# Rotary tables and a norm factor made during the experts, the token update on VectorE alone, and GpSimd given a share of the normalised rows ahead of its low halves

## Chip, cores and metric

One Trainium2 chip; the kernel is one program on one of its cores. The time is device microseconds (us) of one execution, as the median of several. Five engines run at the same time, each through its own instructions in order, and wait for each other by semaphores: TensorE (PE), VectorE (DVE), ScalarE (ACT), GpSimd (POOL) and SyncE (SP), whose queue starts the transfers of the weights.

## The reference, cut

Two transformer-like blocks follow each other on 256 tokens of width 1024, all in float32. The first ends with a mixture of 32 experts; the second begins with a norm, a projection, and rotary tables made from the tokens' positions.

```
def first_block(x, ...):
    ...
        h2 = rmsnorm(x, g_pre_ffn[l]) * (1.0 + sc2) + sh2
        y2 = moe(h2, w_router[l], b_router[l], w_up[l], b_up[l], w_down[l], b_down[l])
        x = x + gt2 * rmsnorm(y2, g_post_ffn[l])
    return x

def rope_tables(positions, rot_dim):
    inv = jnp.power(ROPE_THETA, -(jnp.arange(0, rot_dim, 2, dtype=jnp.float32) / rot_dim))
    ang = positions.astype(jnp.float32)[..., None] * inv
    return jnp.cos(ang)[:, :, None, :], jnp.sin(ang)[:, :, None, :]

def second_block(x, c, positions, ...):
    cos_a, sin_a = rope_tables(positions, ATT_ROT_DIM)
    cos_i, sin_i = rope_tables(positions, IDX_ROT_DIM)
    ...
        mod = jax.nn.silu(c) @ ada_w[l] + ada_b[l]
        shift, scale, gate = jnp.split(mod, 3, axis=-1)
        h = rms_norm(x, norm_g[l]) * (1.0 + scale[:, None, :]) + shift[:, None, :]
        proj = h @ w_in[l]
        (q, k, v, z_att, q_idx, k_idx, w_idx, z_ssm, xbc, dt_raw, gate_logits) = jnp.split(proj, pts, axis=-1)
        ...
        x = x + gate[:, None, :] * (merged @ w_out[l])
```

## The kernel before, in words

**Tokens and weights.** The 256 tokens are two blocks of 128 rows (index i = 0, 1); `xt` holds them, 128 x 2 x 1024. All big weights come in pieces of up to 1 MB through SP's queue, in the order in which they are used, into a ring of buffers; a buffer is filled again when its last reader is done.

**The experts.** A loop over 32 experts e multiplies the tokens that chose e by its two weight matrices. For up to 32 tokens it runs the plain path: eight pieces of `w_up` (`pU`), then the SwiGLU (DVE makes `act`, ACT its tanh `th`, DVE multiplies), then, for expert e - 1, four pieces of `w_down` (`pY`), whose rows DVE and ACT copy to `yz` and PE adds up in `yacc`. If an expert has more than 32 tokens, a branch runs a second chunk of up to 32 right after the SwiGLU (tiles `ov`, `tho`, `pUo`), and if it has more than 64, a third, whose tokens are gathered first (`So` on DVE, `pgo` on PE). Expert 11 takes all three chunks with these inputs.

**The seam.** After the last expert, ACT squares `yacc` and DVE multiplies it by the gate (`yg`). `rstd` computes one over the root of the mean square by DVE alone, with an integer first guess and three Newton steps: a chain of fourteen tiny instructions. Then the tokens are updated, x + rstd * yg: by DVE for three quarters of the columns, and for the last 512 of token block 1 by ACT (scaling) and GpSimd (adding). ACT squares the new tokens for the next norm.

**Block 2** (`block2`) begins with that norm: factor `a3` from the modulation; the first three weight blocks prepared by `early`; a second `rstd`; `norm_rows`, which makes the normalised rows `xn` (in the tile `qkn`), token block 0 by DVE and block 1 by ACT; then, for eight slices k of 128 columns, two PE transposes (`x_T`, tile `pT`) and the two parts of h by `h_halves`: ACT the rounded `h`, DVE `hf` and the remainder `hf` - `h`.

**Splitting.** For float32 accuracy each weight block is split in a rounded high half `wH` (ACT) and a low half `wL` = w - `wH`, and PE makes three products for each. `Flow.halves` decides by a running estimate of loads whether DVE or GpSimd makes a low half. The estimates of both engines start at zero in `block2`, and every instruction that has a price there raises them.

**Order.** `ORDER2` lists the column groups of the projection: first `idx` (the indexer's columns and the step sizes of the state-space part, 324 + 32 columns), then `kv`, `q0` and so on. PE runs them one behind the other. What follows a group runs in "lanes": Python generators that are advanced one step for each weight block, so that their instructions stand between those of the groups. Lane "a" holds first `tables` (the rotary tables `cosin`: eleven table instructions on DVE after a conversion of the positions, and Sin on ACT), then `idx_lane`, which normalises the index key on GpSimd (`kim`, `kiv`, an rsqrt in tile `rsq_t`), applies the rotary tables there, and makes the step sizes (`dtu`, `dtz`). The group `kv` also has a norm, whose rsqrt (`rq`) GpSimd makes behind all of that.

Of the kernel before, what the change touches and what calls it, by code (L numbers as in the profile page):

```python
# [7 lines left out]
F32 = mybir.dt.float32  # L8
F32R = mybir.dt.float32r
BF = mybir.dt.bfloat16  # L10
I32 = mybir.dt.int32
U32 = mybir.dt.uint32
AF = mybir.ActivationFunctionType
OP = mybir.AluOpType
# [6 lines left out]
S, D = 256, 1024  # L21
# [170 lines left out]
class Flow:  # L192
# [11 lines left out]
    def lane(self, q, gen):  # L204
        self.queues[q].append(gen)
# [88 lines left out]
            self.stages()  # L294
        self.pend.clear()

    def early(self, blocks, n, bias=0.0):

        def made():
            for f, w in zip(ws, got):  # L300
                yield None, w
            yield from blocks
        blocks = iter(blocks)
        ws = [next(blocks) for _ in range(n)]
        got = [self.halves(*b) for b in ws]
        for w in got:
            w[0]()
        self.bias, b = bias, self.bias
        for w in got:
            w[1]()  # L310
        self.bias = b
        nop = lambda: None
        got = [(nop, nop, w[2]) for w in got]
        return made()
# [31 lines left out]
def build(tc, A, out):  # L346
    nc = tc.nc
    ACT, SP = nc.scalar, nc.sync
    PE = Load(nc.tensor, PE_PRICES)
    V, G = (Load(e, p, lambda: PE.t) for e, p in ((nc.vector, DVE_PRICES), (nc.gpsimd, POOL_PRICES)))  # L350
    top = ExitStack()
    top.enter_context(tc.manual_schedule())
    con = top.enter_context(tc.tile_pool(name="con", bufs=1))
# [99 lines left out]
    def par(n):  # L453
        return cut(n, (PK, PK0, pk) if n in PK else (PK1, 0, [None, part.get("pk1")]))

    def cs(n):
        return cut(n, (CST, CST0, cst) if n in CST else (CST1, 0, [None, part.get("cst1")]))
# [114 lines left out]
            yield  # L572
        return g

    def norm_rows(xn, x, ss, pool):

        r = pool.tile([128, 2], F32, name="rstd", tag="rstd", bufs=2)
        rstd(r, ss)
        V.tensor_scalar(xn[:, 0], x[:, 0], r[:, 0:1], None, op0=OP.mult)
        ACT.activation(xn[:, 1], x[:, 1], AF.Copy, scale=r[:, 1:2])  # L580

    def x_T(xn, tiles):

# [37 lines left out]
    def blocks(name, ka, extra=None):  # L621

        for j, i in enumerate(at[name]):
            raw = ws.get(i)
            for a in range(ka):
                yield ([raw[:, a]] + ([extra[:, ka * j + a]] if extra is not None else []),
                       (lambda i=i: ws.done(i)) if a == ka - 1 else None)
# [43 lines left out]
        return (lambda: (a[0](), b[0]())), (lambda: (a[1](), b[1]())), lambda: (a[2](), b[2]())  # L671


    def block2(ss=None):
        bk = ExitStack()
        sb = bk.enter_context(tc.tile_pool(name="b2", bufs=1))
# [8 lines left out]
        lane, done, until = fl.lane, fl.done, fl.until  # L685


        a3 = T("a3", [128, 8])
        V.scalar_tensor_tensor(a3, mod2c[:, 8:16], 1.0, par("norm_g2"), op0=OP.add, op1=OP.mult)
        qkn = T("qkn", [128, 16, 256], tag="mg").rearrange("p a b -> p (a b)")[:, :2560].rearrange(  # L690
            "p (i h d) -> p i h d", i=2, h=10)
        xn = qkn.rearrange("p i h d -> p i (h d)")[:, :, :D]
        if ss is None:
            ss = T("ss4", [128, 2])
            for i in range(2):
                ACT.activation(xn[:, i], xt[:, i], AF.Square, accum_out=ss[:, i:i + 1])
        first = fl.early(blocks("idx", 4, par("w_dt").rearrange("p (k c) -> p k c", k=8)), 3, 9.0)
        norm_rows(xn, xt, ss, sb)
        hs = [T(f"h2{i}", [128, 8, 256], F32R) for i in range(2)]

        hk = h_halves(hs, x_T(xn, PG), a3, mod2c[:, 0:8], lambda: T("hf", [128, 512], bufs=2, tag="hjk")[:, :256])


        ri = T("posi", [128, 2], I32)
        ACT.dma_start(ri, A["positions"])
        rp = T("posf", [128, 2])
        cosin = T("cosin", [128, 2, 2, 24])

        def tables():
            V.tensor_copy(rp, ri)  # L710
            ang = T("ang", [128, 2, 24])
            nr = T("nr", [128, 2, 24])
            V.tensor_tensor(ang, cs("invf")[:, None, :].to_broadcast([128, 2, 24]),
                            rp[:, :, None].to_broadcast([128, 2, 24]), op=OP.mult)
            MAGIC = 12582912.0
            V.tensor_scalar(nr, ang, 1.0 / (2.0 * np.pi), MAGIC, op0=OP.mult, op1=OP.add)
            V.tensor_scalar(nr, nr, -MAGIC, None, op0=OP.add)
            c1 = 6.28125
            c2_ = float(np.float32(np.float64(2 * np.pi) - c1))
            c2_ = float(np.float32(np.round(c2_ * 2.0 ** 22) / 2.0 ** 22))  # L720
            c3 = float(2 * np.pi - c1 - c2_)
            for c in (c1, c2_, c3):
                V.scalar_tensor_tensor(ang, nr, -c, ang, op0=OP.mult, op1=OP.add)
            yield
            PI = 3.1415925
            V.tensor_scalar(cosin[:, :, 0], ang, PI, -PI, op0=OP.min, op1=OP.max)
            V.tensor_scalar(ang, ang, float(np.pi / 2), None, op0=OP.add)
            V.tensor_scalar(nr, ang, float(np.pi), float(-2 * np.pi), op0=OP.is_gt, op1=OP.mult)
            V.tensor_tensor(ang, ang, nr, op=OP.add)
            V.tensor_scalar(cosin[:, :, 1], ang, PI, -PI, op0=OP.min, op1=OP.max)  # L730
            yield
            ACT.activation(cosin, cosin, AF.Sin)

        lane("a", tables())

        def rope(x, nh, o, hf):

# [1184 lines left out]
    xn = xq  # L1922
# [94 lines left out]
    def swiglu(U, act, lc, th):  # L2017

        V.tensor_scalar(act, U[:, 0:256], 7.0, None, op0=OP.min)
        V.tensor_scalar(lc, U[:, 256:512], -7.0, 7.0, op0=OP.max, op1=OP.min)  # L2020
        ACT.activation(th, act, AF.Tanh, scale=0.5 * 1.702)  # L2021
        V.scalar_tensor_tensor(act, th, 1.0, act, op0=OP.add, op1=OP.mult)
        V.scalar_tensor_tensor(act, lc, 1.0, act, op0=OP.add, op1=OP.mult)
# [87 lines left out]
    def over_up(e, wu, xT):  # L2111
        with tc.If(rv[e] > 32):  # L2112
            chunk_up(e, lambda k: xT[:, e % 4, k, 32:64], wu, ov[:, 2 * (e % 2)])
            with tc.If(rv[e] > 64):
                x = gather_chunk(e, 2)
                chunk_up(e, lambda k: x[:, k], wu, ov[:, 2 * (e % 2) + 1])
# [29 lines left out]
                far(e, r, b + 1)  # L2146

    aT = {}
    gl = gates_lane()
    for e in range(NE + 1):  # L2150
        if e < NE:
            i0 = at[f"up{e}"][0]
            steps = iter(())
            if e % 4 == 0:
                xT = AR(0, "xT", [128, 4, 8, 64])
                steps = gather(xT, e, min(4, NE - e))
                next(steps)
            U = PU("pU")
            up_bias(e, U)
            act, lc, th = (sb.tile([128, 256], F32, name=n, tag=n, bufs=b) for n, b in (("act", 2), ("lc", 1), ("th", 1)))  # L2160
            if e:
                gs = slots(e - 1, 0, "G", 2)
                next(gs)
            wu = lambda k: ws.get(i0 + k)
            for k in range(8):
                if k % 2 == 0:
                    next(steps, None)
                up_k(U, xT[:, e % 4, k, 0:32], k, wu(k))
                if e == 0 and k < 3:
                    next(gl)  # L2170
                if e and k == 2:
                    g = next(gs)
                if k == 3:
                    rv[e] = nc.values_load(counts[0:1, e:e + 1], engines=(ET.PE, ET.Activation, ET.DVE), min_val=0, max_val=256)
            swiglu(U, act, lc, th)
            over_up(e, wu, xT)
            for j in range(8):
                ws.done(i0 + j)
        if e:
            d0 = at[f"down{e - 1}"][0]  # L2180
            wd = [ws.get(d0 + k) for k in range(4)]
            if e == NE:
                gs = slots(e - 1, 0, "G", 2)
                next(gs)
                g = next(gs)
                gg2, ggc = AR(0, "gg2", [128, D]), sb.tile([128, 8], F32, name="ggc2")
                V.tensor_tensor(ggc, modc[:, 40:48], par("g_post_ffn"), op=OP.mult)
                for _ in row_of(gg2, ggc, at_once(PM)):
                    pass
                over_down(e - 1, wd)  # L2190
            y_out(down(aT[e - 1], wd), yz[e % 2])
        if e < NE:
            aT[e] = sb.tile([128, 2, 128], F32, name="aT", tag="aT", bufs=2)
            act_T(act, aT[e])
        if e:
            scatter(g, yz[e % 2])
            if e < NE:
                over_down(e - 1, wd)
            for k in range(4):
                ws.done(d0 + k)  # L2200
# [13 lines left out]
            V.tensor_tensor(yg[:, i, sl], yacc[i][n], gg2[:, sl], op=OP.mult)  # L2214
    V.tensor_reduce(ss, sq.rearrange("p (i m) -> p i m", m=2), axis=AX.X, op=OP.add)
    rstd(rs, ss)

    q = yg[:, 1, 512:1024]
    ACT.activation(q, q, AF.Copy, scale=rs[:, 1:2])  # L2219
    G.tensor_tensor(xt[:, 1, 512:1024], q, xt[:, 1, 512:1024], op=OP.add)  # L2220
    for i, w in ((0, D), (1, 512)):
        V.scalar_tensor_tensor(xt[:, i, :w], yg[:, i, :w], rs[:, i:i + 1], xt[:, i, :w], op0=OP.mult, op1=OP.add)
        ACT.activation(jk, xt[:, i], AF.Square, accum_out=s3[:, i:i + 1])
    mo.close()
    bx.close()
# [23 lines left out]
```

## Time and profile before

| | us |
|---|---|
| median of 3 runs | 1713.04 |
| lowest and highest run | 1710.18, 1717.36 |
| the profiled execution | 1716.04 |
| its span | 1714.2 |
| PE busy in the span | 1424.8 |
| DVE, ACT, POOL busy | 661.5, 435.9, 271.9 |

The span is what the profiler saw between the first and the last instruction. The experts lie between about 272 and 1270 us of it, where the weights of 32 experts are read; block 2 is what comes behind. The busy shares are means over stages with different limits, so the sections below go by stretches of the span.

### The profile page before, as it was taken

The page shows a single profiled execution, that of the slowest core. Times are in us where ns is not written, and L with a number is a line of the kernel's source. Part 1 is how long each engine was busy: PE and PEld are TensorE (multiplying, and loading weights), DVE is VectorE, ACT ScalarE, POOL GpSimd, SP SyncE. Part 2 cuts the span into 40 slices and gives each one's busy share as a digit, 9 for nine tenths or more (in the row PEclk, how much of TensorE's full clock was granted, in tenths as well). Part 3 has the DMA queues.
Part 4 walks back from the last instruction along what each step waited for, and adds up shares of the span by engine and source line. Part 5 has one row for each costly group of instructions (what it writes and reads, how often), then busy time and mean ns, then how long its engine had stood idle before and what let it go on. Part 6 is the DMA issues. An engine that isn't in the chain of part 4 may idle for free. (4 is left out here: it accounts for less than half of the span.)

```text
span 1714.2 us, 28511 instructions
## 1 busy us (share of the span) xinstructions
PE 1424.8 (83%) x11403; PEld 845.3 (49%) x11403; DVE 661.5 (39%) x1508; ACT 435.9 (25%) x980; POOL 271.9 (16%) x387
## 2 busy tenths in 40 slices
PE   5999988887798898777766778887858888999998
PEld 2775652332233243232132233333227788999996
DVE  3556462121121122121111111221136798766767
ACT  3545331010010011010010010010025555654553
POOL 1127100000000000000000000000005652552533
PEclk8999999999899999889788988999988999999999
DMA  9746896999999988999999998999924344333452
GB/s 377 285 157 219 314 369 267 423 420 422 421 418 420 414 322 353 420 423 421 422 421 421 413 414 336 387 367 420 420 81 148 99 146 144 130 99 113 162 177 91
DMA packets 116487, 526.03 MB, mean 307 GB/s; under 512 B 8744, under 2 KB 11216, under 8 KB 80304
## 3 DMA queue, kind: packets, MB, share of 16 engines
q1 hardware_dynamic: 113392, 518.67, 76.0%
q10 hardware_dynamic: 2496, 3.92, 0.7%
q8 instruction: 157, 2.57, 0.6%
q0 software_dynamic: 384, 0.39, 0.1%
q14 instruction: 58, 0.48, 0.1%
HBM read 521.50 MB, written 1.06 MB: 305 GB/s over the span
## 5 line engine op out<-in xcount | busy, mean ns | idle before, releaser
L145 PE MATMUL pU<-w,xT 128*32 128x512 f32 x2048 | 266.2, 643 | 29.7 <-DMA w<-in_w_up 22.3
L145 PE MATMUL pg<-h,wH 128*128 128x256 f32 x1296 | 249.4, 292 | 9.8 <-ACT wH L254 3.1
L145 DVE TENSOR_TENSOR wL<-w,wH 128x512 fp32r<-128x512 f32 (+2 forms) x244 | 174.2, 728 | 111.1 <-PE pg L145 59.4
L145 PEld LDWEIGHTS pg<-h,wH 128*128 128x128 f32 x1296 | 205.5, 195 | 23.3 <-issue 7.0
L145 PE MATMUL pY<-w,aT 128*32 128x256 f32 x2048 | 151.2, 445 | 73.1 <-PEq L2112 41.3
L254 ACT CAST wH<-w 128x512 fp32r<-128x512 f32 (+4 forms) x312 | 176.1, 587 | 116.0 <-PE pg L145 101.7
L145 PE MATMUL pg<-h,wL 128*128 128x256 f32 (+1 forms) x648 | 186.2, 287 | 6.3 <-DVE wL L145 3.7
L145 POOL TENSOR_TENSOR xt<-yg,xt 128x512 f32<-128x512 f32 x1 | 1.5, 1485 | 1025.9 <-ACT yg L2219 1025.9
L145 PEld LDWEIGHTS pY<-w,aT 128*32 128x32 f32 x2048 | 79.3, 125 | 157.2 <-issue 74.8
L145 PEld LDWEIGHTS pU<-w,xT 128*32 128x32 f32 x2048 | 62.7, 115 | 171.9 <-issue 114.8
L145 DVE COPY yz<-pY 32x256 f32<-32x256 f32 x94 | 39.2, 417 | 248.6 <-PE pY L145 227.6
L145 PEld LDWEIGHTS pg<-h,wL 128*128 128x128 f32 (+1 forms) x648 | 125.7, 194 | 8.0 <-DVE wL L145 4.8
L145 POOL TENSOR_TENSOR wL<-w,wH 128x512 fp32r<-128x512 f32 (+2 forms) x68 | 87.8, 1297 | 222.6 <-PE pg L145 135.7
L2064 ACT COPY yz<-pY 32x256 f32<-32x256 f32 x94 | 34.1, 363 | 304.4 <-DVE yz L145 304.4
L145 PE MATMUL yacc<-yz,G 64*128 64x512 f32 x256 | 91.9, 627 | 17.8 <-ACT yz L2064 17.8
L2021 ACT ACTIVATE th<-act 128x256 f32<-128x256 f32 x32 | 13.3, 416 | 357.8 <-DVE act L145 357.8
L145 PE MATMUL pUo<-w,xT 128*32 128x512 f32 x832 | 92.1, 595 | 0.0
L145 DVE COPY G<-pG 128x256 f32<-128x256 f32 x32 | 13.6, 424 | 183.9 <-PE pG L145 183.9
L145 DVE TENSOR_SCALAR act<-pU 128x256 f32<-128x256 f32 x32 | 13.6, 424 | 155.5 <-PE pU L145 155.5
L145 PE MATMUL pg<-wH,h 128*128 128x512 f32 (+2 forms) x224 | 69.4, 393 | 3.6 <-ACT wH L254 1.9
L145 PE MATMUL pg<-yk,wH 128*128 128x256 f32 x384 | 68.6, 281 | 0.1
L145 PE MATMUL pY<-w,aTo 128*32 128x256 f32 x960 | 54.9, 380 | 9.1 <-DVE Go L145 8.5
(451 smaller groups left out, 1950.1 us busy)
## 6 DMA issues: line engine op xcount, KB each, us to landing
w<-in_w_up SPq DMA_DIRECT2D x256, 1024.0 KB, 17.3
w<-in_w_down SPq DMA_DIRECT2D x128, 1024.0 KB, 19.7
w<-in_w_in SPq DMA_DIRECT2D x48, 1024.0 KB, 4.9
w<-in_w_ada SPq DMA_DIRECT2D x24, 1024.0 KB, 8.5
w<-in_ada_w SPq DMA_DIRECT2D x12, 1024.0 KB, 6.7
w<-in_w_out SPq DMA_DIRECT2D x8, 1024.0 KB, 4.9
w<-in_w_branch_ssm SPq DMA_DIRECT2D x8, 1024.0 KB, 4.9
w<-in_w_branch_att SPq DMA_DIRECT2D x4, 1024.0 KB, 4.9
```

The lines of the kernel that those rows point to most:

```text
L145: return f(*a, **k)
L254: self.nc.scalar.copy(H[:, a:b], p)
L2021: ACT.activation(th, act, AF.Tanh, scale=0.5 * 1.702)
L2064: (ACT.copy if q % 2 else V.tensor_copy)(y[o:o + 32, c:c + 256], t[o:o + 32, 0:256])
```

## The change

Four edits. (1) The factor `a3` and the rotary tables move out of `block2` into a generator `tables`, which the expert loop advances after the SwiGLU of experts 9, 10 and 11: in 9 the factor and the load of the positions, in 10 the first half of the table arithmetic, in 11 the second half and Sin. (2) The token update is made by DVE alone, two instructions of 1024 columns. (3) `norm_rows` is called inside `early`, between the high halves and the low halves of the first three blocks. (4) The last 256 columns of token block 1 are normalised by GpSimd; ACT does 768.

```diff
-    def early(self, blocks, n, bias=0.0):
+    def early(self, blocks, n, bias=0.0, between=None):
...
         for w in got:
             w[0]()
+        if between:
+            between()
         self.bias, b = bias, self.bias
         for w in got:
             w[1]()
...
-    def norm_rows(xn, x, ss, pool):
+    def norm_rows(xn, x, ss, pool, third=0):
...
         V.tensor_scalar(xn[:, 0], x[:, 0], r[:, 0:1], None, op0=OP.mult)
-        ACT.activation(xn[:, 1], x[:, 1], AF.Copy, scale=r[:, 1:2])
+        ACT.activation(xn[:, 1, :D - third], x[:, 1, :D - third], AF.Copy, scale=r[:, 1:2])
+        if third:
+            G.tensor_scalar(xn[:, 1, D - third:], x[:, 1, D - third:], r[:, 1:2], None, op0=OP.mult)
...
+    def tables(pool):
...
+        V.scalar_tensor_tensor(a3, mod2c[:, 8:16], 1.0, par("norm_g2"), op0=OP.add, op1=OP.mult)
...
+        ACT.dma_start(ri, A["positions"])
+        yield
+        V.tensor_copy(rp, ri)
...
+        for c in (c1, c2_, c3):
+            V.scalar_tensor_tensor(ang, nr, -c, ang, op0=OP.mult, op1=OP.add)
+        yield
...
+        V.tensor_scalar(cosin[:, :, 1], ang, PI, -PI, op0=OP.min, op1=OP.max)
+        ACT.activation(cosin, cosin, AF.Sin)
...
-        a3 = T("a3", [128, 8])
-        V.scalar_tensor_tensor(a3, mod2c[:, 8:16], 1.0, par("norm_g2"), op0=OP.add, op1=OP.mult)
...
-        first = fl.early(blocks("idx", 4, par("w_dt").rearrange("p (k c) -> p k c", k=8)), 3, 9.0)
-        norm_rows(xn, xt, ss, sb)
+        first = fl.early(blocks("idx", 4, par("w_dt").rearrange("p (k c) -> p k c", k=8)), 3, 9.0,
+                         lambda: norm_rows(xn, xt, ss, sb, 256))
...
-        lane("a", tables())
...
-    gl = gates_lane()
+    gl, tb = gates_lane(), tables(sb)
...
             swiglu(U, act, lc, th)
+            if e > 8:
+                next(tb, None)
             over_up(e, wu, xT)
...
-    q = yg[:, 1, 512:1024]
-    ACT.activation(q, q, AF.Copy, scale=rs[:, 1:2])
-    G.tensor_tensor(xt[:, 1, 512:1024], q, xt[:, 1, 512:1024], op=OP.add)
-    for i, w in ((0, D), (1, 512)):
-        V.scalar_tensor_tensor(xt[:, i, :w], yg[:, i, :w], rs[:, i:i + 1], xt[:, i, :w], op0=OP.mult, op1=OP.add)
+    for i in R:
+        V.scalar_tensor_tensor(xt[:, i], yg[:, i], rs[:, i:i + 1], xt[:, i], op0=OP.mult, op1=OP.add)
         ACT.activation(jk, xt[:, i], AF.Square, accum_out=s3[:, i:i + 1])
```

The program's instructions by engine show where this puts them. GpSimd at the seam, before (its last instruction of the token update, then the low halves of the first three blocks; `pk1` holds the 32 extra columns):

```order
L145 TENSOR_TENSOR xt_71<-yg_42332,xt_71 128x512
L145 TENSOR_TENSOR wL_42391<-w438_14681,wH_42382 128x324
L145 TENSOR_TENSOR wL_42391<-pk1__66,wH_42382 128x32
L145 TENSOR_TENSOR wL_42394<-w438_14681,wH_42383 128x324
L145 TENSOR_TENSOR wL_42394<-pk1__66,wH_42383 128x32
L145 TENSOR_TENSOR wL_42397<-w438_14681,wH_42384 128x324
L145 TENSOR_TENSOR wL_42397<-pk1__66,wH_42384 128x32
```

and with the change, where its first instruction is its share of the normalised rows, which reads `rstd`:

```order
L145 TENSOR_SCALAR qkn_42398<-xt_71,rstd_42408 128x256
L145 TENSOR_TENSOR wL_42427<-w438_14702,wH_42399 128x324
L145 TENSOR_TENSOR wL_42427<-pk1__66,wH_42399 128x32
L145 TENSOR_TENSOR wL_42430<-w438_14702,wH_42400 128x324
L145 TENSOR_TENSOR wL_42430<-pk1__66,wH_42400 128x32
L145 TENSOR_TENSOR wL_42433<-w438_14702,wH_42401 128x324
L145 TENSOR_TENSOR wL_42433<-pk1__66,wH_42401 128x32
```

The low halves have moved behind an instruction that waits for the norm's `rstd`.

DVE among the rows of h, before (from the fourth slice on; the table instructions stand between the slices):

```order
L145 TENSOR_SCALAR hf_42449<-pT_42450,a3_42379,mod2c_77 128x256
L145 TENSOR_TENSOR h21_42419<-hf_42449,h20_42418 128x256
L145 CAST posf_42422<-posi_42420 128x2
L145 TENSOR_TENSOR ang_42468<-cst1__68,posf_42422 128x48
L145 TENSOR_SCALAR nr_42469<-ang_42468 128x48
L145 TENSOR_SCALAR nr_42469<-nr_42469 128x48
L145 SCALAR_TENSOR_TENSOR ang_42468<-nr_42469,ang_42468 128x48 x3
L145 TENSOR_SCALAR hf_42476<-pT_42477,a3_42379,mod2c_77 128x256
L145 TENSOR_TENSOR h21_42419<-hf_42476,h20_42418 128x256
L145 TENSOR_SCALAR cosin_42423<-ang_42468 128x2x24
L145 TENSOR_SCALAR ang_42468<-ang_42468 128x48
L145 TENSOR_SCALAR nr_42469<-ang_42468 128x48
```

and with the change, from the fourth slice on to the end of the group's rows:

```order
L145 TENSOR_SCALAR hf_42463<-pT_42464,a3_79,mod2c_77 128x256
L145 TENSOR_TENSOR h21_42437<-hf_42463,h20_42436 128x256
L145 TENSOR_SCALAR hf_42481<-pT_42482,a3_79,mod2c_77 128x256
L145 TENSOR_TENSOR h21_42437<-hf_42481,h20_42436 128x256
L145 TENSOR_SCALAR hf_42502<-pT_42503,a3_79,mod2c_77 128x256
L145 TENSOR_TENSOR h21_42437<-hf_42502,h20_42436 128x256
L145 TENSOR_SCALAR hf_42521<-pT_42522,a3_79,mod2c_77 128x256
L145 TENSOR_TENSOR h21_42437<-hf_42521,h20_42436 128x256
L145 TENSOR_SCALAR hf_42540<-pT_42541,a3_79,mod2c_77 128x256
L145 TENSOR_TENSOR h21_42437<-hf_42540,h20_42436 128x256
L145 TENSOR_TENSOR wL_42550<-w439_14860,wH_42528 128x324
L145 TENSOR_TENSOR wL_42550<-pk1__66,wH_42528 128x32
```

The tables are gone from there, and a low half of 324 and 32 columns, which GpSimd made before, stands on DVE behind the last slice.

ACT in expert 11, before (`th` is the plain path's tanh, `tho` the second and third chunk's, both tanh too):

```order
L2021 ACTIVATE th_6646<-act_6644 128x256
L2112 COMPARE_AND_BRANCH
L2021 ACTIVATE tho_6743<-ov_2463 128x256
L2114 COMPARE_AND_BRANCH
L2089 ACTIVATE xo_6751<-pgo_6754,modc_76,a2_282 128x32 x4
L2021 ACTIVATE tho_6833<-ov_2463 128x256
L2114 UNCONDITIONAL_BRANCH x2
L2112 UNCONDITIONAL_BRANCH
L2064 COPY yz1_2458<-pY_6855 32x256 x2
```

and with the change:

```order
L2022 ACTIVATE th_6661<-act_6659 128x256
L708 ACT_TABLE_LOAD
L708 ACTIVATE cosin_80<-cosin_80 128x96
L2113 COMPARE_AND_BRANCH
L2022 ACT_TABLE_LOAD
L2022 ACTIVATE tho_6764<-ov_2465 128x256
L2115 COMPARE_AND_BRANCH
L2090 ACTIVATE xo_6772<-pgo_6775,modc_76,a2_284 128x32 x4
L2022 ACTIVATE tho_6854<-ov_2465 128x256
L2115 UNCONDITIONAL_BRANCH x2
L2113 UNCONDITIONAL_BRANCH
L2065 ACT_TABLE_LOAD
```

Sin and three loads of function tables have come in: ahead of Sin, ahead of the second chunk's tanh, and ahead of the copies to `yz`. Two table loads of block 2, ahead of Sin and ahead of the Exp of `dtu`, have gone.

## Rows read from the trace of the kernel before

**Rows 1.** Waits of PE from 1260 us to the end: total, times, longest.
```profile
PE pT L145 <- DVE qkn L145: 16.9, 1, 16.9
...
PE pT L145 <- DVE hf L145: 2.8, 2, 2.3
```

**Rows 2.** Waits of ACT, 1300 to 1350 us: total, times, longest.
```profile
ACT qkn L883 <- POOL rq L145: 12.3, 2, 6.9
```

**Rows 3.** Timeline of DVE, 1276 to 1288 us: start, busy, instruction (xcount).
```profile
1277.07 0.17 DVE L145 TENSOR_SCALAR ss<-ss 128x2 f32<-128x2 f32 x1
...
1278.85 2.96 DVE L145 SCALAR_TENSOR_TENSOR xt<-yg,rs,xt 128x1024 f32<-128x1024 f32 x2
...
1283.10 0.17 DVE L145 SCALAR_TENSOR_TENSOR a<-mod2c,pk__66 128x8 f32<-128x8 f32 x1 [1.30 <-ACT jk L2223]
...
1283.19 0.16 DVE L145 TENSOR_SCALAR ss<-ss 128x2 f32<-128x2 f32 x1
...
1287.03 0.75 DVE L145 TENSOR_SCALAR qkn<-xt,rstd 128x1024 f32<-128x1024 f32 x1
```

**Rows 4.** Timeline of POOL, 1270 to 1322 us.
```profile
1279.77 1.49 POOL L145 TENSOR_TENSOR xt<-yg,xt 128x512 f32<-128x512 f32 x1 [1025.86 <-ACT yg L2219]
...
1283.50 0.87 POOL L145 TENSOR_TENSOR wL<-w,wH 128x324 fp32r<-128x324 f32 x1 [2.25 <-ACT wH L254]
...
1292.49 0.89 POOL L145 TENSOR_TENSOR wL<-w,wH 128x324 fp32r<-128x324 f32 x1 [5.85 <-PE pg L145]
```

**Rows 5.** Timeline of ACT, 1270 to 1322 us: the squares of the norm.
```profile
1281.19 0.18 ACT L2223 ACTIVATION_READ_ACCUMULATOR jk<-xt 128x1 f32 x1
...
1281.92 1.06 ACT L2223 ACTIVATE jk<-xt 128x1024 f32<-128x1024 f32 x1 [0.55 <-DVE xt L145]
```

**Rows 6.** Timeline of PE, 1270 to 1322 us.
```profile
1287.98 2.17 PE L145 MATMUL pT<-cst__67,qkn 128*128 128x128 f32 x8 [16.94 <-DVE qkn L145]
```

**Rows 7.** Windows: us, busy (xcount) by engine, granted clock, DMA share, GB/s.
```profile
1299.00:1302.00 3.00, 3.00 (x11) 3.00 (x12) 2.93 (x7) 2.32 (x7) 2.04 (x4) 0.50 0.00 0
```

**Rows 8.** Timeline of DVE, 1270 to 1322 us: the rows of h and the tables.
```profile
1290.08 0.43 DVE L145 TENSOR_TENSOR h<-hf,h 128x256 fp32r<-128x256 f32 x1
...
1292.83 0.82 DVE L145 TENSOR_TENSOR h<-hf,h 128x256 fp32r<-128x256 f32 x1
...
1293.58 0.21 DVE L145 CAST posf<-posi 128x2 f32<-128x2 int32 x1
```

**Rows 9.** Timeline of ACT, 1270 to 1322 us: the second table load.
```profile
1306.04 1.28 ACT L776 ACT_TABLE_LOAD   x1
1307.33 0.26 ACT L776 ACTIVATE dtu<-dtu 128x64 f32<-128x64 f32 x1
```

**Rows 10.** Timeline of DVE, 1306 to 1309 us.
```profile
1306.90 0.28 DVE L145 TENSOR_REDUCE kim<-idx 128x2 f32<-128x128 f32 x1
1307.62 0.41 DVE L145 TENSOR_SCALAR dtz<-dtu 128x64 f32<-128x64 f32 x1 [0.44 <-ACT dtu L776]
```

**Rows 11.** Lines of POOL by form, 1307 to 1347 us: busy, mean ns, idle before.
```profile
L145 POOL TENSOR_TENSOR rsq_t<-rsq_t,kiv 128x2 f32<-128x2 f32 x3 | 1.1, 375 | 0.2
...
L145 POOL TENSOR_TENSOR rsq_t<-rsq_t,hn 128x4 f32<-128x4 f32 x3 | 0.6, 200 | 0.2
```

**Rows 12.** Timeline of ACT in expert 11, 500 to 640 us.
```profile
598.82 0.42 ACT L2021 ACTIVATE tho<-ov 128x256 f32<-128x256 f32 x1 [6.67 <-DVE ov L145]
```

**Rows 13.** Timeline of PE in expert 11, 586 to 640 us.
```profile
600.45 5.05 PE L145 MATMUL pgo<-So,xh 128*128 128x32 f32 x32 [2.22 <-DVE So L145]
```

**Rows 14.** Windows over expert 11.
```profile
590.00:632.00 42.00, 37.02 (x337) 17.28 (x330) 9.81 (x27) 4.96 (x13) 0.00 (x0) 0.92 0.84 330
```

**Rows 15.** One ACT line over the whole span: duration, first and last start.
```profile
L2021 ACT ACTIVATE th<-act x32: 416/416/418, 272.8 to 1226.7; 128x256 f32<-128x256 f32 x32
```

**Rows 16.** DMA issues, 1200 to 1400 us: count, size, median us to landing.
```profile
posi<-in_positions ACTq DMA_DIRECT2D x1, 1.0 KB, 1.7
...
w<-in_w_down SPq DMA_DIRECT2D x8, 1024.0 KB, 20.0
```

More of the change, by code (lines that the diff above doesn't have):

```diff
@@ L671, in both @@
         return (lambda: (a[0](), b[0]())), (lambda: (a[1](), b[1]())), lambda: (a[2](), b[2]())
+    a3 = con.tile([128, 8], F32, name="a3")
+    cosin = con.tile([128, 2, 2, 24], F32, name="cosin")
+    def tables(pool):
+        T = lambda name, shape, dt=F32: pool.tile(shape, dt, name=name)
+        V.scalar_tensor_tensor(a3, mod2c[:, 8:16], 1.0, par("norm_g2"), op0=OP.add, op1=OP.mult)
+        ri, rp, ang, nr = T("posi", [128, 2], I32), T("posf", [128, 2]), T("ang", [128, 2, 24]), T("nr", [128, 2, 24])
+        ACT.dma_start(ri, A["positions"])
+        yield
+        V.tensor_copy(rp, ri)
+        V.tensor_tensor(ang, cs("invf")[:, None, :].to_broadcast([128, 2, 24]),
+                        rp[:, :, None].to_broadcast([128, 2, 24]), op=OP.mult)
+        MAGIC = 12582912.0
+        V.tensor_scalar(nr, ang, 1.0 / (2.0 * np.pi), MAGIC, op0=OP.mult, op1=OP.add)
+        V.tensor_scalar(nr, nr, -MAGIC, None, op0=OP.add)
+        c1 = 6.28125
+        c2_ = float(np.float32(np.float64(2 * np.pi) - c1))
+        c2_ = float(np.float32(np.round(c2_ * 2.0 ** 22) / 2.0 ** 22))
+        c3 = float(2 * np.pi - c1 - c2_)
+        for c in (c1, c2_, c3):
+            V.scalar_tensor_tensor(ang, nr, -c, ang, op0=OP.mult, op1=OP.add)
+        yield
+        PI = 3.1415925
+        V.tensor_scalar(cosin[:, :, 0], ang, PI, -PI, op0=OP.min, op1=OP.max)
+        V.tensor_scalar(ang, ang, float(np.pi / 2), None, op0=OP.add)
+        V.tensor_scalar(nr, ang, float(np.pi), float(-2 * np.pi), op0=OP.is_gt, op1=OP.mult)
+        V.tensor_tensor(ang, ang, nr, op=OP.add)
+        V.tensor_scalar(cosin[:, :, 1], ang, PI, -PI, op0=OP.min, op1=OP.max)
+        ACT.activation(cosin, cosin, AF.Sin)
     def block2(ss=None):
@@ L696, in block2 @@
                 ACT.activation(xn[:, i], xt[:, i], AF.Square, accum_out=ss[:, i:i + 1])
-        first = fl.early(blocks("idx", 4, par("w_dt").rearrange("p (k c) -> p k c", k=8)), 3, 9.0)
-        norm_rows(xn, xt, ss, sb)
+        first = fl.early(blocks("idx", 4, par("w_dt").rearrange("p (k c) -> p k c", k=8)), 3, 9.0,
+                         lambda: norm_rows(xn, xt, ss, sb, 256))
         hs = [T(f"h2{i}", [128, 8, 256], F32R) for i in range(2)]
         hk = h_halves(hs, x_T(xn, PG), a3, mod2c[:, 0:8], lambda: T("hf", [128, 512], bufs=2, tag="hjk")[:, :256])
[L704 to L732, printed above, removed]
-        lane("a", tables())
         def rope(x, nh, o, hf):
```

## The prediction

> **What bounds the kernel now.** I read the waits of TensorE (PE) over the last part first, because the page shows a program of two halves, and all that the change edits lies where one half hands over to the other. PE stands still for 16.9 us at that seam, the longest single wait of the whole end, until the normalised rows (tile qkn) are there; a little later it stands twice more, 2.8 us together, for VectorE's instruction hf [rows 1]. So the seam is a serial chain on the other engines, and a microsecond cut from it is a microsecond of time, if nothing behind it takes it back. The waits of ScalarE (ACT) say what is behind: twice, 12.3 us in all, it stands for the tile rq, which GpSimd (POOL) makes at the end of a long serial run of small instructions that begins with the index columns [rows 2]. ACT works in order, so the weights' high halves queue behind that wait and PE follows. The end of the program therefore moves with the moment at which the index group hands its columns to GpSimd, not with PE's own speed: that moment is what I price. Then I read the timelines of VectorE (DVE), POOL and ACT through the seam.
>
> **Token update.** Two DVE instructions of 1024 and 512 columns start at 1278.85 and are busy for 2.96 us, to 1281.81 [rows 3]. GpSimd's add runs from 1279.77 to 1281.26 [rows 4], and the half-width one ends only 0.55 us after it: it was held. At 0.55 for 512 columns, two free full-width ones take about 2.2 us and end near 1281.1. ACT's second square then no longer waits for them but for the read of the first accumulator, which ends at 1281.37; it started at 1281.92 before [rows 5]. Gain **0.5** (0.3 to 0.55). The ACT scaling and the GpSimd add that go were beside DVE's first instruction and return nothing by themselves.
>
> **Norm's factors and GpSimd's place.** The factor a stands in front of the norm's first instruction, 1283.10 against 1283.19: **0.1** when it has gone [rows 3]. From that instruction (ss) to the rows (qkn) DVE takes 3.84 us, 1283.19 to 1287.03. The same chain of tiny instructions in the token update took 1.78 us, 1277.07 to 1278.85 [rows 3]. What differs is GpSimd, which starts its six low-half instructions at 1283.50 [rows 4]. In the new order its first instruction waits for the end of that chain, so the chain runs free: gain **2.05**. GpSimd's own share (256 of 1024 columns of one token block) costs PE nothing: it is read only by the last two of eight pairs of transposes. ACT's shorter share gives nothing either, since PE waits for DVE first. The danger is that GpSimd's share starts before DVE's qkn: DVE would then wait for it. GpSimd's 324-column low of two inputs takes 0.87 [rows 4], so 256 columns of one input are at most 0.7: low bound 1.35. I take no loss, as DVE needs no semaphore from another engine to go on.
>
> [...]
>
> **Rotary tables.** They stand on DVE between the fourth and the last rows of h, from 1293.58 [rows 8], and their Sin on ACT waits for them. PE's 2.8 us for hf are this [rows 1]. [...] Against it stand the lows. GpSimd's first three now run after its share of the rows, beside DVE's first h, each of which can lose 0.4 (0.82 against 0.43, [rows 8]); PE sees little of it, since its first block still runs at half clock. The planner also counts the share as GpSimd's load and gives DVE the seventh low, behind the last h, 324 and 32 columns: about 0.65 where PE is waiting next. I take 0.8 for both (0 to 1.6). Gain **3.5** (2.7 to 4.3). How late the transposes themselves start (1287.98, [rows 6]) is in the terms above.
>
> **Table loads.** At 1306.04 ACT loads the table of Exp for 1.28 us, because Sin has thrown it out; DVE's dtz waits for the result until 1307.62 and could start when kim ends, 1307.18 [rows 9, 10]. GpSimd's chain waits for DVE behind it. With Sin gone there is no load here: gain **0.4** (0 to 0.44). Sin's own load was inside the wait counted above.
>
> The three loads move into expert 11. The first and the last run while ACT idles (it waits 6.67 us before tho, [rows 12]). The middle one carries the wait for ov, so it starts only when ov is there and delays tho by 1.28. Behind tho on DVE stands So, and PE waits for So already now, 2.22 us [rows 13]. This expert keeps the DMA engines only 0.84 busy, at 330 GB/s [rows 14]: PE sets the pace, and the weights' stream moves back with it. Toll **-1.3** (0 if the stream makes it up).
>
> [...]
>
> **Other moves.** The table arithmetic on DVE in experts 10 and 11, a dozen instructions of about 0.2 us (posf 0.21, [rows 8]), fills an idle stretch: between an expert's act and its ov ACT idles for 6.67 us, and DVE with it [rows 12]. Without that cover it would cost 2 to 3 us. The load of the positions is issued by ACT in expert 9; SP's queue keeps its order.
>
> **Sum.** 0.5 + 0.1 + 2.05 + 3.5 + 0.4 - 1.3 = 5.3 us (bounds 3.2 and 7.4). The profiled execution took 1716.04 us, its span 1714.2; this gives 1710.7. It lies 3.0 over the median of 1713.04, on which I predict **1707.7**.
>
> **Rivals.**
> A, more than the sum: no toll in expert 11 and no loss to the lows (7.4), and GpSimd's chain, shifted against DVE's lows, collides less. Its twelve instructions of the first rsqrt (four forms, three of each) average up to 0.375, and 0.200 where DVE is idle [rows 11]: 12 x 0.175 = 2.1. Gain 9.5, 1703.5. For it: the chain does start 0.4 earlier against PE's pace. Against it: DVE's lows come at PE's pace either way.
> B, given back: the bounds at their low ends (3.2), and the same collisions growing by as much, 2.1. Gain about 1, 1712. For it: more of GpSimd's lows now lie beside DVE's h. Against it: the tables, which were held by the same lows, are gone.
> C, slower: the positions' load lands late. An expert lasts (1226.7 - 272.8) / 31 = 30.8 us [rows 15]; DVE converts the positions in order, one expert after their issue, with 6.7 us to spare. Up to 37.5 us nothing is lost; from 43 us the change loses all it gained, from 51 it is over 0.5% slower, 1722. A weight piece of 1 MB needs 20.0 us in that stage, but the positions are 1 KB on a queue of their own and took 1.7 us at the quiet seam [rows 16].
> That it does nothing, the gain of the seam being hidden, would need slack behind the index group; ACT's 12.3 us of waiting for GpSimd [rows 2] show none.
>
> **Numbers.** The forecast gets 0.52 (its own range 1705.6 to 1709.8), A 0.20, B 0.24, C 0.04. About 0.5%, 8.6 us, is what a measurement of this kernel can tell from no change. The forecast and B lie within it, A just beyond: faster 0.20, same 0.77, slower 0.03. The range, 1703.0 to 1712.0, takes in A and B.
>
> **What would show it.** Right: no gap of 0.55 us between the two squares; 1.8 us from ss to qkn; qkn about 2.6 us earlier after the last scatter; no PE wait for hf and no half clock after it; no table load behind the index columns; the index group over some 6 us earlier against the last scatter; an ACT wait for rq that is as long as before. In expert 11 a table load between ov and tho, and PE's wait for So near 3.5 us. Wrong: qkn on DVE stretched to 1.4 us by GpSimd's share; PE waiting for a low of DVE at the end of the index group for over 1.5 us; a GpSimd chain from kim to rq that is 2 us longer; a late posf.

## The result and the profile after

The changed kernel takes 1724.03 us (median of 6, 1721.33 to 1728.82) where the kernel before took 1713.9 (6 runs): ratio 1.0064, 95% interval 1.0042 to 1.0085. It is slower by 11 us by the ratio; the prediction said 5.3 faster. Its profiled execution took 1722.86, span 1721.0.

The seam went much as forecast. The timeline of the kernel after, all engines, in the columns of [rows 3]:

```profile
1288.08 2.85 DVE L145 TENSOR_TENSOR yg<-yacc,gg 128x512 f32<-128x512 f32 x4 [5.61 <-ACT jk L2216]
...
1292.81 2.48 DVE L145 SCALAR_TENSOR_TENSOR xt<-yg,rs,xt 128x1024 f32<-128x1024 f32 x2
1296.56 0.17 DVE L145 TENSOR_SCALAR ss<-ss 128x2 f32<-128x2 f32 x1 [1.27 <-ACT jk L2222]
1297.44 0.17 DVE L145 TENSOR_SCALAR rstd<-ss 128x2 int32<-128x2 int32 x1 [0.72 <-DVE ss L145]
1297.65 0.35 DVE L145 SCALAR_TENSOR_TENSOR rstd_h<-rstd,ss 128x1 f32<-128x1 f32 x2
...
1299.02 0.75 DVE L145 TENSOR_SCALAR qkn<-xt,rstd 128x1024 f32<-128x1024 f32 x1
...
1299.26 0.94 ACT L583 ACTIVATE qkn<-xt,rstd 128x768 f32<-128x768 f32 x1 [1.30 <-issue]
1299.44 1.13 POOL L145 TENSOR_SCALAR qkn<-xt,rstd 128x256 f32<-128x256 f32 x1 [1045.37 <-DVE rstd L145]
...
1300.08 1.94 PE L145 MATMUL pT<-cst__67,qkn 128*128 128x128 f32 x8 [15.17 <-DVE qkn L145]
```

The waits there: ScalarE's for rq (1309 to 1360 us) is 1.8 shorter than in [rows 2], TensorE's for the rows is 1.7 shorter than in [rows 1], and its matmuls' wait for hf is gone from the list.

```profile
ACT qkn L884 <- POOL rq L145: 10.5, 2, 5.6
PE pT L145 <- DVE qkn L145: 15.2, 1, 15.2
```

To compare stretches of two executions I count from the start of the last yg (1274.12 before, 1288.08 after). To the end of the span it is 440.1 us before and 432.9 after: 7.2 us were gained behind the experts. So the loss lies ahead of the seam, and is larger than the result: 14.0 us in these two executions. The last expert's activation starts 13.4 us later than in [rows 15], though the first starts 1.0 earlier:

```profile
L2022 ACT ACTIVATE th<-act x32: 416/417/418, 271.8 to 1240.1; 128x256 f32<-128x256 f32 x32
```

Two windows in which the DMA engines are busy throughout say what is slower. The kernel before, and then the one after (us; busy time of PE, PEld, DVE, ACT, POOL; granted clock; DMA share; GB/s):

```profile
300.00:500.00 200.00, 163.84 (x1438) 65.51 (x1440) 37.33 (x94) 18.21 (x45) 0.00 (x0) 0.93 1.01 421
700.00:900.00 200.00, 148.30 (x1170) 56.90 (x1174) 31.40 (x79) 16.21 (x39) 0.00 (x0) 0.85 1.02 422
```

```profile
300.00:500.00 200.00, 162.78 (x1415) 64.32 (x1418) 37.34 (x94) 18.17 (x44) 0.00 (x0) 0.91 1.02 415
700.00:900.00 200.00, 145.22 (x1144) 56.56 (x1140) 32.48 (x82) 16.09 (x39) 0.00 (x0) 0.82 1.02 415
```

The DMA engines are as busy as before and move 1.5% less. The first window ends before the change puts anything into the experts (its first step is in expert 9, at 535 us). The pieces are the same, and so are packets and bytes, but for one packet of 116,488. What differs in the program is where the buffers lie, the parts of the on-chip memory (SBUF) into which the pieces of the weights are loaded. `a3` (32 bytes in each partition) and `cosin` (384) are now made in the pool of constants, and everything allocated behind it moves up by 416 bytes. The fifteen buffers that the experts' weights go through start at

| | first pool (4) and second pool (6) | five at the right end of SBUF |
|---|---|---|
| before | multiples of 512 (35328, ...) | 480 past a multiple (188384, ...) |
| after | 416 past a multiple (35744, ...) | 480 past a multiple |

**Theory of place:** transfers into a buffer that doesn't start at some round address are slower. **Theory of the added work:** what was put into experts 9 to 11 costs it.

### The profile page after: what moved, and what is told of

Same layout as the page of the kernel before. It is cut to its first block, busy times and chain, and to the rows that moved or that the text cites. A ratio compares the mean times of both kernels' runs of the same rounds, so it can differ in the third digit from the quotient of the medians.

```text
span 1721.0 us, 28509 instructions
## 1 busy us (share of the span) xinstructions
PE 1427.9 (83%) x11403; PEld 843.1 (49%) x11403; DVE 658.1 (38%) x1510; ACT 436.6 (25%) x980; POOL 271.2 (16%) x385
```

## The experiments

All ratios are against the kernel before, run beside them on the same chip. The e1 to e4, the e5 to e9, the f and the g versions ran on four chips, so versions of different sets are compared by their ratios, whose intervals are 2 to 4 us to either side. "GB/s" are those of 300 to 500 and 700 to 900 us; "off" counts the buffers of fifteen that don't start at a multiple of 256 bytes (the limit is found below).

| version | off | median us | ratio (95%) | GB/s |
|---|---|---|---|---|
| before | 5 | 1712 to 1714 | 1 | 421, 422 |
| after | 15 | 1724.03 | 1.0064 (1.0042 to 1.0085) | 415, 415 |
| e1 after, ten at 512 | 5 | 1710.13 | 0.9994 (0.9981 to 1.0007) | 419, 422 |
| e2 before, a3 and cosin moved | 15 | 1729.29 | 1.0096 (1.0074 to 1.0118) | 414, 415 |
| e3 before, ten 64 past | 15 | 1725.91 | 1.0082 (1.0061 to 1.0103) | 414, 414 |
| e6 before, ten 128 past | 15 | 1726.52 | 1.0086 (1.0064 to 1.0107) | 415, 415 |
| e7 after, ten 256 past | 5 | 1710.90 | 1.0001 (0.9986 to 1.0015) | 421, 421 |
| e4 after, all at 512 | 0 | 1708.22 | 0.9974 (0.9960 to 0.9989) | 422, 423 |
| e9 e1, tables and a3 behind the experts | 5 | 1709.89 | 0.9989 (0.9976 to 1.0001) | 420, 422 |
| e5 e4, sine in expert 12 | 0 | 1705.25 | 0.9962 (0.9949 to 0.9975) | 419, 422 |
| f1 e5, right five 128 past | 5 | 1708.63 | 0.9962 (0.9947 to 0.9977) | 421, 422 |
| f2 e5, no GpSimd share | 0 | 1707.32 | 0.9962 (0.9946 to 0.9978) | 422, 423 |
| f3 e5, low halves first | 0 | 1708.49 | 0.9961 (0.9945 to 0.9978) | 420, 422 |
| f4 before, right five at 512 | 0 | 1711.81 | 0.9988 (0.9972 to 1.0004) | 422, 423 |
| g2 e5, first four 128 past | 4 | 1703.90 | 0.9946 (0.9928 to 0.9963) | 422, 422 |
| g1 e5, six 128 past | 6 | 1708.53 | 0.9978 (0.9961 to 0.9995) | 422, 422 |
| g4 e5, ten 128 past | 10 | 1712.55 | 1.0004 (0.9985 to 1.0024) | 419, 420 |
| g3 e5, all 128 past | 15 | 1721.61 | 1.0054 (1.0033 to 1.0075) | 415, 415 |

**Place or added work (e1, e2).** e1 pads the constants of the changed kernel to a shift of 512; e2 moves the two tiles in the kernel before and nothing else.

```diff
 # e1, in the kernel after
+    pad = con.tile([128, 24], F32, name="pad")
     a3 = con.tile([128, 8], F32, name="a3")
 # e2, in the kernel before, ahead of block2 (their lines in block2 go)
+    a3 = con.tile([128, 8], F32, name="a3")
+    cosin = con.tile([128, 2, 2, 24], F32, name="cosin")
```

> The changed kernel with 96 unused bytes more per partition among the constants, so that the ten weight buffers behind them start at multiples of 512 bytes again, as before the change. Theory of place (the transfers into SBUF are slower where a buffer starts 32 bytes off a multiple of 64): the stream of weights moves at 421 to 422 GB/s again instead of 415 in 300 to 500 us and 700 to 900 us, the last expert's th starts near 1228 us instead of 1240.1, and the time is 1707 to 1710 us (the 7 us gained behind the experts and the toll of 1.3 in expert 11 are kept). Theory of the added work (tables, their load and ScalarE's two function tables in experts 9 to 11 cost it): nothing changes, 1722 to 1726 us, 415 GB/s.

> The kernel before, with nothing changed but that a3 and cosin, 416 bytes, are made among the constants, so that the weight buffers lie as in the changed kernel. Theory of place: 415 GB/s, the last expert's th starts 11 to 13 us later than 1226.7, and the time is 1725 to 1729 us. Theory of the added work: as before, 1712 to 1716 us and 421 GB/s.

Both came out as the theory of place has it: e2 does none of the added work and is as slow as the changed kernel, or slower; e1 does all of it and is not slower than before. One miss: in e2's profiled execution, its lowest (1721.15), the last th started only 3.2 us later than in [rows 15], not 11 (its first started 4.7 earlier); its GB/s are those of the theory. The windows of e2, then of e1:

```profile
300.00:500.00 200.00, 165.38 (x1443) 64.77 (x1446) 38.31 (x97) 18.34 (x45) 0.00 (x0) 0.92 1.02 414
700.00:900.00 200.00, 145.78 (x1146) 57.17 (x1142) 31.40 (x79) 16.23 (x39) 0.00 (x0) 0.83 1.02 415
```

```profile
300.00:500.00 200.00, 166.48 (x1457) 66.63 (x1458) 38.95 (x98) 18.56 (x45) 0.00 (x0) 0.93 1.01 419
700.00:900.00 200.00, 145.61 (x1166) 56.34 (x1170) 31.41 (x79) 16.21 (x39) 0.00 (x0) 0.85 1.02 422
```

**Which address is round enough (e3, e6, e7).** Pads of 64 and 128 bytes before, and of 352 (a shift of 768) after.

```diff
 # e3 / e6, in the kernel before, ahead of block2
+    pad = con.tile([128, 16], F32, name="pad")   # e6: [128, 32]
 # e7, as e1 with
+    pad = con.tile([128, 88], F32, name="pad")
```

> The kernel before with 64 unused bytes among the constants: the ten buffers start 64 bytes behind a multiple of 512. If a multiple of 64 is what a transfer wants: as before, 1712 to 1716 us and 421 GB/s. If it is a multiple of 128, 256 or 512: slower, near 1726 us and 415 GB/s. Theory of the added work: as before.

> The kernel before with 128 unused bytes among the constants: the ten buffers start 128 bytes behind a multiple of 512. If a multiple of 128 is enough for the full rate: 421 to 422 GB/s in 700 to 900 us and 1711 to 1716 us. If it takes 256 or 512: 414 to 415 GB/s and 1724 to 1730 us, as with 64.

> The changed kernel with 352 unused bytes among the constants: the ten buffers start 256 bytes behind a multiple of 512. If a multiple of 256 is enough: 421 to 422 GB/s in 700 to 900 us and 1708 to 1712 us, as with 512. If it takes 512: 414 to 415 GB/s and 1722 to 1727 us.

The windows of e3, e6 and e7 in that order, one fence each:

```profile
700.00:900.00 200.00, 145.19 (x1152) 56.46 (x1153) 33.01 (x83) 16.65 (x40) 0.00 (x0) 0.84 1.02 414
```

```profile
700.00:900.00 200.00, 147.63 (x1146) 56.90 (x1144) 32.99 (x83) 16.65 (x40) 0.00 (x0) 0.83 1.02 415
```

```profile
700.00:900.00 200.00, 147.40 (x1154) 56.44 (x1146) 31.40 (x79) 16.21 (x39) 0.00 (x0) 0.84 1.02 421
```

64 and 128 bytes past cost about as much as 416 past (14 and 15 us by the ratios, 128 on two runs only); 256 past costs nothing that is measured. Of the offsets tried for the ten, only multiples of 256 kept the rate: 421 and 422 GB/s in 700 to 900 us (e7, e1), against 414 at 64 past and 415 at 128 and at 416 past. Why the others are slower is not shown.

**How much each buffer costs (e4, f4, f1, g1, g2, g4, g3).** A gap above the five right-hand buffers (480 bytes puts them at multiples of 512, 352 at 128 past), one between the two pools, and pads of the constants. e4 is e1 with the gap, f4 the kernel before with it; the others are made in e5, which is e4 with the tables one expert later (its edit is shown further down).

```diff
 # e4, f4 (f1: [128, 88])
+        bx.enter_context(tc.tile_pool(name="gap", bufs=1, side="right")).tile([128, 120], F32, name="gap")
         wB = bx.enter_context(tc.tile_pool(name="wB", bufs=1, side="right"))
 # g1, g2
+    big.enter_context(tc.tile_pool(name="gap2", bufs=1)).tile([128, 32], F32, name="gap2")
     ar = big.enter_context(tc.tile_pool(name="ar", bufs=1))
 # g2, g3, g4 (g3 with f1's gap)
-    pad = con.tile([128, 24], F32, name="pad")
+    pad = con.tile([128, 56], F32, name="pad")
```

> As the first of these, and besides 480 unused bytes above the five weight buffers at the right end of SBUF, which start 32 bytes off a multiple of 64 in both kernels: now all fifteen start at multiples of 512. Theory of place: if ten moved buffers cost 13 us, five give about half of that, 6 us: 424 to 425 GB/s and 1700 to 1704 us. Theory of the added work: as the changed kernel, 1722 to 1726 us.

> The kernel before, with nothing changed but 480 unused bytes above the five buffers at the right end, so that all fifteen start at multiples of 512. From the pair of runs of the changed kernel with and without it: 2 us less than before, 1710 to 1711 us, 422 to 423 GB/s. If these five buffers cost in proportion to the ten: 6 us less, 1706 us.

> The best version so far (all fifteen buffers at multiples of 512 bytes, the sine in expert 12), but with the five buffers at the right end of SBUF 128 bytes behind a multiple of 512. If a buffer 128 bytes off costs its transfers the same wherever it lies: five of fifteen cost half of what ten cost (13 to 15 us), so 1711 to 1713 us and 419 to 420 GB/s in 700 to 900 us. If these five matter little, as in the two runs in which they were 480 bytes off (2 us): 1706 to 1708 us and 422 GB/s.

> The best version so far with only the four buffers of the first pool 128 bytes behind a multiple of 512 (the six of the second are at 256, which had the full rate). In proportion: 1710 to 1712 us and 420 GB/s. If only where most are off: 1705 to 1708 us and 422 GB/s.

> The best version so far (1705 us) with only the six buffers of the second pool 128 bytes behind a multiple of 512, nine buffers at multiples. Cost in proportion to the buffers' number (1.3 to 1.5 us for each): 1713 to 1714 us and 418 to 420 GB/s in 300 to 500 and 700 to 900 us. A cost that only shows when most buffers are off: 1705 to 1708 us and 422 GB/s.

> The best version so far with the ten buffers of both pools 128 bytes behind a multiple of 512 and the five at the right end at multiples. By the theory of place: 13 to 15 us more, 1718 to 1720 us, 415 GB/s. If the five at the right end do count, 416 to 417 GB/s and 1716 to 1718 us, better than the runs with fifteen off.

> The best version so far with all fifteen buffers 128 bytes behind a multiple of 512. If the five at the right end cost little wherever the others lie: the same as with ten off, 1718 to 1720 us, 415 GB/s. If each buffer off adds its part once the transfers of most are slowed: 1722 to 1726 us, 412 GB/s.

Expecting a cost per buffer was wrong for the first few. At 1.2 to 1.6 us for each, as the ten of e1 and e2 have it, five buffers would cost 6 to 8; measured are 3.4 (e4 against e1 by the ratios), 2.1 (f4 against the kernel before, an interval that takes in none) and none (f1 against e5). In the series on e5, four off cost nothing and six 2.7 us (1.6 permille), within the noise of e5, though g1 and g2, beside each other, are 5.5 apart with intervals that barely touch. Ten cost 7.2 us (1.0004 - 0.9962, times 1713), less than either expectation for g4, and fifteen 15.8. The last step is the cleanest: g3 differs from g4 in the start of the five right-hand buffers and of no other tile, and they cost 8.6 there. The windows of g1, g4, g3:

```profile
700.00:900.00 200.00, 146.76 (x1176) 57.37 (x1168) 31.40 (x79) 16.24 (x39) 0.00 (x0) 0.85 1.02 422
```

```profile
700.00:900.00 200.00, 147.93 (x1138) 55.83 (x1134) 31.40 (x79) 16.21 (x39) 0.00 (x0) 0.82 1.02 420
```

```profile
700.00:900.00 200.00, 147.01 (x1146) 57.39 (x1146) 31.41 (x79) 16.24 (x39) 0.00 (x0) 0.82 1.02 415
```

The packets show the same form. Of the packets of 8 KB that the traces have between 300 and 1200 us, 97 to 98% took 309 ns with no buffer off (e4, e5, f4), 96 to 97% with four to six at 128 past (f1, g1, g2), 90% with the right-hand five at 480 past (before, e1, e7), 81% with ten off (g4) and 22 to 42% with fifteen off, where the median is 312 to 313 ns. So most packets into a buffer that is off take no longer as long as few are off.

So the change, which took the count from five to fifteen, went over the steep part. Why the first few cost so little is not shown.

**The toll of the tables (e5, e9).** e5 starts them one expert later; e9 puts them back behind the experts, and with them, contrary to its expectation, the instruction that makes a3 (0.1 us by the prediction).

```diff
 # e5
-            if e > 8:
+            if e > 9:
                 next(tb, None)
 # e9, in e1: no call in the experts; a yield ahead of Sin; in block2, ahead of the norm, then behind h_halves
+        V.scalar_tensor_tensor(a3, mod2c[:, 8:16], 1.0, par("norm_g2"), op0=OP.add, op1=OP.mult)
...
+        tb = tables(sb)
+        next(tb)
+        lane("a", tb)
```

> The version with all fifteen weight buffers at multiples of 512 bytes, and the tables' three steps one expert later: the sine in expert 12, whose activation is not followed by one for rows beyond 32. Theory of the toll (2.9 us in expert 11: 1.3 for the table load ahead of tho and 1.6 for the product behind it at a lower granted clock): from expert 11's th to expert 12's 52.8 us as before instead of 55.7, nothing lost in expert 12, the time 2.5 to 3 us below the version with the sine in expert 11, 1704 to 1706 us. Rival (the two loads are hidden under the weights' transfers, which wait for nobody): the same time as there, 1708 us.

> The changed kernel with its ten buffers at multiples of 512 again and the tables computed behind the experts as before the change; a3, the token update and GpSimd's share as changed. By the prediction's terms: the gain of 3.5 for the tables goes, the toll in expert 11 goes with it (2.9 by the traces), so 0.5 to 1 us more than with the tables in the experts, 1710 to 1712 us; from the last yg to the end 437 us instead of 433.9, and TensorE waits for hf again. Rival (the tables were worth nothing, and the 7 us behind the experts come from the norm's factors alone): 433.9 us from the last yg to the end, and 1706 to 1708 us.

In the changed kernel, expert 11 on ScalarE, and TensorE's product there:

```profile
594.16 1.28 ACT L708 ACT_TABLE_LOAD   x1
...
600.80 1.28 ACT L2022 ACT_TABLE_LOAD   x1 [4.41 <-DVE ov L145]
602.09 0.42 ACT L2022 ACTIVATE tho<-ov 128x256 f32<-128x256 f32 x1
...
603.73 6.49 PE L145 MATMUL pgo<-So,xh 128*128 128x32 f32 x32 [3.50 <-DVE So L145]
...
620.62 1.28 ACT L2065 ACT_TABLE_LOAD   x1
```

TensorE waits 3.50 for So instead of the 2.22 of [rows 13], the 1.28 that was forecast. The same 32 products then took 6.49 instead of 5.05, at a granted clock of 0.60 (603 to 609 us; 0.71 from 600 to 606 before). That isn't the tables' doing. e6, the kernel before with nothing but a pad, has the old wait and as slow a product:

```profile
603.43 6.79 PE L145 MATMUL pgo<-So,xh 128*128 128x32 f32 x32 [2.22 <-DVE So L145]
```

From expert 11's th to expert 12's it is 52.8 us before and in most versions without the sine there, and 54.4 in e6 and f4; with the sine in expert 11 it is 54.0 in e4 and e7, and 55.7 in the changed kernel and e1. In the four long ones of these, e6, f4, the changed kernel and e1, TensorE was at the lower granted clock, 0.50, for 10.2 us of that expert, in all others for 6.8. So the toll is 1.25 at either, and the 1.6 of the clock come with and without the tables: in two of four executions with the sine there and two of fourteen without, too few to say whether the tables make them likelier. In e5 it is 52.8 again, and two loads stand in expert 12, where nobody waits:

```profile
638.15 0.42 ACT L2024 ACTIVATE th<-act 128x256 f32<-128x256 f32 x1 [2.97 <-DVE act L145]
638.59 1.28 ACT L709 ACT_TABLE_LOAD   x1
640.91 1.28 ACT L2067 ACT_TABLE_LOAD   x1
```

e5 is 2 us under e4 by the ratios, which is within their intervals. In e9 the wait for hf is back, and the last yg to the end takes 439.1 instead of 431.9 to 434.7 in the kernels with the tables in the experts and the seam as changed. Yet e9's time is no longer than e1's or e7's; what gives the 5 us back is not found. The wait, and the clock behind it:

```profile
PE pT L145 <- DVE hf L145: 2.1, 2, 1.6
```

```profile
1295.46:1298.46 3.00, 2.91 (x16) 2.21 (x14) 2.97 (x7) 2.20 (x6) 2.81 (x4) 1.00 0.27 40
```

The half clock of [rows 7] isn't there, though the wait is. At the same place behind the last yg it shows in three of the six executions with that wait (before, e6, f4) and not in the other three (e2, e3, e9).

**GpSimd's share and its place (f2, f3).**

```diff
 # f2
-                         lambda: norm_rows(xn, xt, ss, sb, 256))
+                         lambda: norm_rows(xn, xt, ss, sb))
 # f3
-        first = fl.early(blocks(...), 3, 9.0,
-                         lambda: norm_rows(xn, xt, ss, sb, 256))
+        first = fl.early(blocks(...), 3, 9.0)
+        norm_rows(xn, xt, ss, sb, 256)
```

> The best version so far without GpSimd's share of the normalised rows: ScalarE does all 1024 columns again, 1.15 us instead of 0.94. GpSimd's 256 columns took 1.13 us and ended 0.4 us after ScalarE's 768, so by the traces the share gains nothing: first transposes at the same time or 0.2 us earlier behind the last yg, the time 1704 to 1707 us. By the prediction's term the share was worth 0.2 to 0.4 us: the first transposes later by that.

> The best version so far with the norm's factors and rows written behind the first three blocks' low halves again, as before the change. By the prediction's term: from ss to qkn 3.8 us instead of 2.5, since GpSimd's low halves run beside VectorE's small instructions, and GpSimd's share behind them, so the first transposes 1.4 to 2.5 us later and the time 1706 to 1708 us. Rival (ss to qkn is long for another reason): 2.5 us, no change in time.

The timeline of f2:

```profile
1283.25 0.17 DVE L145 TENSOR_SCALAR ss<-ss 128x2 f32<-128x2 f32 x1 [1.27 <-ACT jk L2224]
...
1283.65 0.87 POOL L145 TENSOR_TENSOR wL<-w,wH 128x324 fp32r<-128x324 f32 x1 [1030.62 <-ACT wH L254]
...
1284.58 0.99 DVE L145 SCALAR_TENSOR_TENSOR rstd_h<-rstd,ss 128x1 f32<-128x1 f32 x2
...
1285.70 1.11 DVE L145 SCALAR_TENSOR_TENSOR rstd_h<-rstd,ss 128x1 f32<-128x1 f32 x2
...
1287.38 0.75 DVE L145 TENSOR_SCALAR qkn<-xt,rstd 128x1024 f32<-128x1024 f32 x1
```

My expectation for f2 was wrong in an instructive way: the share is worth having for something else than its own work. It waits for rstd, and GpSimd takes it first, so it keeps the low halves behind it from running beside the chain. Without it they start at 1283.65 and pairs of tiny instructions take 0.99 and 1.11 instead of 0.35; ss to qkn is 4.13 instead of 2.46, and the same 4.12 in f3. Both lose 1.7 us at the first transposes. The times don't show it (0.9962 and 0.9961 against 0.9962), but their intervals, 2.7 us to either side, couldn't. In f3's trace the 1.7 stand for 110 us and are gone by the tile qT; f3 and f1 then differ by 0.2 to 1.7 from place to place and end alike, 434.5 and 434.6 from yg. f2's trace keeps 1.4 to the end, 436.0.

## Why the prediction was wrong, step by step

- **The step that failed is "Other moves"**, and the sum that rests on it. It priced the instructions that move and took the experts' stream for unchanged ("SP's queue keeps its order"), a term put at nothing for that reason alone. The order stayed; the rate didn't. The move of two small tiles into the constants shifted ten of the weight buffers, so that all fifteen now start off multiples of 256 bytes. By e1 that costs 12 us (1.0064 - 0.9994, times 1713), by e2 16. This is shown from both sides, with and without the rest of the change. The diff shows the two `con.tile` lines; the prediction names neither.
- **Token update and the factor a**, forecast 0.5 + 0.1: from the last yg to ss 9.07 before, 8.48 after, 0.59. Right.
- **Norm's factors**, forecast 2.05: ss to qkn went from 3.84 [rows 3] to 2.46, so 1.4. The chain runs free, as said: without an idle 0.72 between ss and rstd it takes 1.74, the forecast 1.8. The idle is new (0.34 in e2 and e9, none in e3, e6 and f4); its cause stays open. The danger named there, GpSimd ahead of qkn, didn't come: its share started 0.42 behind, and took 1.13, not at most 0.7.
- **Rotary tables and Exp load**, forecast 3.5 + 0.4: against e9, e7 is ahead by 1.6 us at TensorE's first product of 512 columns (25.7 against 27.3 after the last yg), by 2.7 ten us later, and by 5.0 at the end. Right in kind; the size is not better known than that. Of the term, 1.5 stood for the half clock behind the wait for hf: an estimate, half of the 3.00 us busy of [rows 7], that no run shows by itself. What the runs show: this half clock is there in only half of the executions with that wait, and behind the wait a pair of the products of 128 x 356 takes 0.80 us where it is there (before, e6, f4) and 0.48 where it isn't (e2, e3, e9). DVE did get the seventh low, and PE waited 0.66 for it at 1311.45, as priced.
- **Toll**, forecast 1.3: 1.25, at either length of the lower clock. Right. No more than the load's 1.28 shows: tho starts at 602.09, 1.29 after the load's start at 600.80.
- **The seam as a whole** came out in sum as forecast, in part by luck, with the norm's term too large and the tables' too small: the terms add up to 6.55, and from the last yg to the end five traces with the seam as before have 440.1 to 441.6, ten with it as changed 431.9 to 434.7, 6.7 less in the mean.
- **Sum without the place:** 5.3 was forecast. At equal places the ratios give, as the gain of the change's own work, 1 us (e1, between 3.3 faster and 1.2 slower) and none (e7) with five buffers off, 2.4 with none off (e4 against f4) and 3.1 to 5.5 with fifteen off (the changed kernel against e3, e6 and e2), the last two with 4 to 5 us to either side. None shows it clearly slower by itself, but how much of the seam's gain, less the toll, arrives in the time stays open; by e1 and e7 it is less than forecast, and e9 says the same of the tables. Single executions scatter by 7.
- **Rival C** had the right sign for the wrong reason: the positions landed 7.3 us after their issue and were converted 29.8 after it, with time to spare.

**A version that beats both** is e5, 1705.25 (0.9949 to 0.9975): the change, all buffers at multiples of 256 bytes, the sine in an expert without a second chunk. f1, f2, f3 and g2 are not told apart from it.

## What to carry to other kernels

When a change adds or moves even a small tile in a pool that others are stacked on, look up where the big transfers' buffers start before and after: here 416 bytes of constants cost more than all of the change's work gained. Price a moved instruction also by what it holds back on its engine. A gain at a hand-over counts only if nothing behind takes it back: of 1.7 us lost at the first transposes, one trace kept 1.4 to the end and the other none. And before a slower clock is put down to a change, look for it in runs without the change: here the low clock of expert 11 was in both.

## What the runs showed of the hardware

- Transfers into SBUF buffers that start 64, 128 or 416 bytes past a multiple of 512 moved 414 to 415 GB/s in the window 700 to 900 us with all fifteen buffers off, 421 to 423 with at most six off; with ten at 256 past it was 421 (e7), with the same ten at 0 it was 422 (e1). The count of packets, the bytes and the DMA engines' busy share (1.02) don't show it; the time of a packet of 8 KB does, with a median of 312 to 313 ns against 309.
- The cost isn't proportional: up to six of 15 off cost at most 3.4 us against none off, ten 7 and fifteen 16.
- Beside GpSimd's low halves, pairs of VectorE's tiny instructions took 0.99 and 1.11 us (f2) instead of the 0.35 without (the changed kernel).
- The same 32 products of 128 x 32 took 4.6 to 6.8 us: 5.05 at a granted clock of 0.71 (before, 600 to 606 us) and 6.49 at 0.60 (after, 603 to 609 us); 5.05 and 6.79 behind the same wait of 2.22, 5.57 and 6.49 behind 3.50.
